# One-bank accumulators and four raw weight tiles in the MLP of an encoder layer

## The chip, the cores and the metric

The kernel runs on one core of a Trainium2 chip, in float32. TensorE (PE) multiplies; VectorE (DVE), ScalarE (ACT) and GpSimd (POOL) read and write tiles in on-chip memory; SyncE (SP) issues most of the DMA transfers, in the order of its queue. Each engine takes its instructions in order and waits on semaphores that other engines set. Accumulators lie in PSUM, which holds eight banks of 128 x 512 floats. The metric is the device time of one execution, in microseconds, as the median of several runs.

## The reference

One layer of an encoder over 1024 tokens of width 1024: windowed attention and a two-way SSD branch, merged by gates; cross attention; a squared-ReLU MLP of width 4096; a last RMSNorm. The change touches what follows the cross attention:

```python
    h = rmsnorm(x, norm_ffn[i])
    x = x + jnp.square(jax.nn.relu(h @ w_up[i])) @ w_down[i]
return rmsnorm(x, norm_final)
```

## The kernel before

**Precision.** Every product is made in three passes: an operand is split in a high part (ACT copies it in a rounded type) and a low part (the difference, by POOL or DVE), and PE adds high x high, high x low and low x high. `put` (L1071) splits one 128 x 512 piece of weights so: ACT at L1073, POOL at L1074; its result is a tile `wop`, of which there are six.

**The up projection** makes u = relu(h @ w_up) squared, 1024 x 4096, in 16 blocks of 256 columns. A block is a 2 x 2 product of halves (tokens, depth, columns), made with seven products in place of eight, in the manner of Strassen and Winograd. The left operands are `a11`, `a12`, `a22` and four sums `s1` to `s4`, made once. The right ones are sums of the block's raw weights b11, b21, b12, b22, which come by DMA in two tiles `raw` of 128 x 1024 (L1079, two buffers). `weights(b)` (L1082) makes them: DVE forms w0 and w1 (L1089, L1090), then overwrites w1 (L1096) and w0 (L1093) when `put` has read them. Each of the seven products is 12 matmuls of 128 x 128 by 128 x 512 (`product`, L1100).

**Order.** From the MLP on, PE's order is the order of the code; the other engines' order, and that of SP's queue, is set by a scheduler. The stage has three parts:

- *Products ahead* (`ahead`, L1117): for blocks 0 to 7 products 1 and 2 are made while the rows of h still come in, between the last units of the cross attention's output projection (`xops`), the transposes of rows (`nt`) and the sums (`sums`, L1033). Product 1 is copied to `x` (ACT, L1126) and stored; product 2 is added to it (DVE, L1129) for the quarter c11, and `square` (L1108) stores that. `x` is needed again later.
- *Whole quads* (`quad`, L1133): blocks 8 to 15, products 1, 2, 6, 5, 7, 3, 4. Product 1 is copied to c11 (ACT, L1147), product 2 added (DVE, L1149). Products 6, 7 and 4 add up in `pb`, products 5 and 3 in `pc`, each copied or added out between (L1153 to L1175).
- *Early quads*: blocks 0 to 7 in the same function, without products 1 and 2; `x` comes back by DMA (L1143). Product 6 in pb is added to x by DVE (c12, L1154) before product 7 adds on in the same tile. The last quarter c21 is L1171.

While quad n runs, the weights of quad n + 1 are made. In the last three rounds of the loop (n = 13 to 15 and behind it) the four u tiles and four tiles of w_down for the first block of the down projection are fetched (`uraw`, `draw`) and split (L1002 to L1014) into freed tiles `kt`. These raw rows lie in tiles of the tag `ld` (two buffers), which until the products ahead hold normalised rows `xn`.

**Accumulators.** Pool `pg` has two tiles of two banks each, pool `pp` four of one bank. In a block, `pc` and `pd` (products 5 and 2) are the halves of one two-bank tile, named `pcd`; in the products ahead the two products are its halves too. A wait is for a tile: who writes a half waits for the readers of that tile before it, whichever half they read. `pb`, `nt`, `xops` and, in the down projection, `dps` are of pool `pp`.

**The down projection** (L1179) adds u @ w_down to x in eight blocks over depth; a unit of 12 matmuls fills one `dps` tile, which DVE adds to the row (`xl`, L1215).

## Time and profile before

| | us |
|---|---|
| median of 3 runs | 2543.43 (2537.66 to 2545.66) |
| the profiled execution | 2546.5 |
| its span, first to last instruction | 2544.7, granted TensorE clock 0.984 on average |
| PE busy | 2421.6 (95%) |
| DVE, ACT, POOL busy | 1337.0, 1072.0, 1055.8 |
| products ahead, from the first product to the first whole quad | 1792.01 to 1876.55 |
| whole quads | to 2046.09 |
| early quads | to 2185.62 |
| down projection and last norm | to the end |

In rows of PE's timeline stand the start, the duration, the line and operation, the output and inputs by name, the number of matmuls taken together, and in brackets the idle time before with the engine and line that ended it. A matmul's duration includes its way through the array, so that rows overlap a little. PEclk is the share of the full clock that TensorE was granted. A list of waits gives for each line the engine and line that it waited for, the total, the number and the longest.

### The profile page before, as it was taken

To read this page: it belongs to the slowest core of one execution; us is meant where nothing else is said; L and a number is where in the kernel's file an instruction comes from. 1 tells how busy PE (TensorE), PEld (TensorE's weight loads), DVE (VectorE), ACT (ScalarE), POOL (GpSimd) and SP (SyncE) were. 2 spreads that over 40 slices of the span, in tenths; PEclk is the share of its full clock that TensorE was granted. 3 is DMA by queue.
4 is the path that set the end of the run, shared out by engine and by line. 5 is a ranking of instruction groups with operands and counts; after the bars stand their busy time and mean duration, and the time that the engine had idled before them with its cause. 6 is when DMAs were issued, how large, how long until landed. Compare 5 with 4: busy or idle time off the path is not lost.

```text
span 2544.7 us, 32517 instructions
## 1 busy us (share of the span) xinstructions
PE 2421.6 (95%) x12156; PEld 2002.4 (79%) x12156; DVE 1337.0 (53%) x2048; ACT 1072.0 (42%) x2214; POOL 1055.8 (41%) x905
## 2 busy tenths in 40 slices
PE   7899999999999999999999999999889998999998
PEld 6788887887878778777778788888767776788887
DVE  5747657576565752665552423236644465454443
ACT  5436445464453643776752422235433332221211
POOL 4234536345363442554444443244745544231210
PEclk9999999999999999999999999999989999999999
DMA  6213224132231311111153535122423344432211
GB/s 221 84 61 113 81 77 123 52 116 72 81 112 64 121 60 65 50 45 48 40 196 128 207 132 199 50 83 84 131 94 107 100 165 145 153 132 83 84 65 67
DMA packets 154926, 260.47 MB, mean 102 GB/s; under 512 B 11792, under 2 KB 86672, under 8 KB 154768
## 3 DMA queue, kind: packets, MB, share of 16 engines
q1 hardware_dynamic: 83872, 219.58, 25.3%
q10 hardware_dynamic: 70896, 38.81, 5.4%
q8 instruction: 96, 1.57, 0.2%
q14 instruction: 62, 0.51, 0.1%
HBM read 210.90 MB, written 47.45 MB: 102 GB/s over the span
## 4 chain that ended last, share of the span: by engine, by line
PE 62%; DVE 12%; POOL 8%; ACT 7%; issue 6%; DMA 4%; SPq 0%; ACTq 0%; POOLq 0%; DVEq 0%
PE dps L81 4%; PE dps L85 4%; PE dps L86 4%; PE pcd L1105 4%; PE pb L1105 4%; PE mps L86 3%; PE mps L85 3%; PE mps L81 3%; PE zp L85 2%; PE zp L81 2%; PE zp L86 2%; DMA raw<-in_wup_dram 2%; PE st L462 2%; POOL prev L477 1%; DVE cx L350 1%
## 5 line engine op out<-in xcount | busy, mean ns | idle before, releaser
L67 POOL TENSOR_TENSOR wlo<-raw,whi 128x1024 fp32r<-128x1024 f32 x142 | 349.8, 2464 | 599.0 <-ACT whi L66 566.4
L66 ACT ACTIVATE whi<-raw 128x1024 fp32r<-128x1024 f32 x144 | 152.0, 1055 | 257.6 <-PE mps L85 116.3
L81 PE MATMUL cps<-kt,whi 128*128 128x512 f32 x512 | 217.5, 425 | 8.6 <-DVE cx L350 8.6
L86 PE MATMUL cps<-kt,wlo 128*128 128x512 f32 x512 | 201.7, 394 | 0.0
L85 PE MATMUL cps<-kt,whi 128*128 128x512 f32 x512 | 201.4, 393 | 0.0
L1074 POOL TENSOR_TENSOR wop<-w,wop 128x512 fp32r<-128x512 f32 x64 | 92.1, 1445 | 117.6 <-ACT wop L1073 117.6
L81 PEld LDWEIGHTS cps<-kt,whi 128*128 128x128 f32 x512 | 97.4, 190 | 34.8 <-issue 16.0
L85 PEld LDWEIGHTS cps<-kt,whi 128*128 128x128 f32 x512 | 97.5, 191 | 26.1 <-issue 7.0
L86 PEld LDWEIGHTS cps<-kt,wlo 128*128 128x128 f32 x512 | 97.4, 190 | 21.1
L81 PE MATMUL gps<-kt,whi 128*128 128x512 f32 x256 | 109.6, 428 | 0.0
L120 POOL TENSOR_TENSOR rr<-rv,mhalf 128x1 f32<-128x1 f32 (+1 forms) x50 | 38.6, 772 | 171.1 <-DVE rv L118 165.7
L496 ACT ACTIVATE ef<-rows,ebias 128x128 f32<-128x128 f32 x256 | 83.2, 391 | 53.3 <-PE cb L511 49.6
L86 PE MATMUL mps<-yk,wlo 128*128 128x512 f32 x256 | 100.5, 393 | 4.8 <-POOL wlo L67 4.8
L680 POOL TENSOR_SCALAR t<-t,den 128x384 f32<-128x384 f32 (+1 forms) x128 | 69.2, 561 | 81.9 <-DVE den L678 73.7
L81 PE MATMUL dps<-kt 128*128 128x512 f32 x256 | 99.7, 390 | 2.7 <-DVE xl L1215 2.7
L86 PE MATMUL gps<-kt,wlo 128*128 128x512 f32 x256 | 101.8, 398 | 0.0
L1105 PE MATMUL pcd<-s,wop 128*128 128x512 f32 x384 | 95.9, 398 | 5.8 <-DVE c L1149 5.5
L85 PE MATMUL mps<-yk,whi 128*128 128x512 f32 x256 | 100.4, 392 | 0.8 <-DVE yk L734 0.8
L85 PE MATMUL gps<-kt,whi 128*128 128x512 f32 x256 | 101.2, 395 | 0.0
L81 PE MATMUL mps<-yk,whi 128*128 128x512 f32 x256 | 100.5, 393 | 0.0
L85 PE MATMUL dps<-kt 128*128 128x512 f32 x256 | 99.6, 389 | 0.0
L86 PE MATMUL dps<-kt 128*128 128x512 f32 x256 | 99.6, 389 | 0.0
(369 smaller groups left out, 7130.5 us busy)
## 6 DMA issues: line engine op xcount, KB each, us to landing
rows<-d_cs ACTq DMA_DIRECT2D x128, 256.0 KB, 3.8
raw<-in_wssd_dram SPq DMA_DIRECT2D x48, 512.0 KB, 3.3
raw<-in_wup_dram SPq DMA_DIRECT2D x40, 512.0 KB, 3.6
raw<-in_wsb_dram SPq DMA_DIRECT2D x32, 512.0 KB, 3.2
d_u<-c SPq DMA_DIRECT2D x64, 256.0 KB, 2.7
uraw<-d_u SPq DMA_DIRECT2D x32, 512.0 KB, 4.2
raw<-in_wdn_dram SPq DMA_DIRECT2D x28, 512.0 KB, 4.2
x<-in_x_dram SPq DMA_DIRECT2D x16, 512.0 KB, 6.4
```

Of the source, the lines that this page charges most:

```text
L66: nc.scalar.activation(hi, raw, AF.Copy)
L67: (eng or nc.gpsimd).tensor_tensor(lo, raw, hi.bitcast(F32), ALU.subtract)
L81: i = mm(out, l[0], r[0], start=first, stop=False)
L85: mm(out, l[0], r[1], start=False, stop=False)
L86: mm(out, l[1], r[0], start=False, stop=last)
L120: nc.gpsimd.tensor_tensor(r[:, :n], v[:, :n], kx.mhalf[:, :n], ALU.pow)
L350: V.scalar_tensor_tensor(acc[:, :S - o], ps[:, o:], cw(k), acc[:, :S - o], ALU.mult, ALU.add)
L462: PE.matmul(st[:, lo:hi], q.btok[:, c], xs.rearrange("p d h q -> p (d h q)")[:, lo:hi], start=True, stop=True)
L496: A.activation(ef[:, h], rows[:, 0, h], AF.Exp, bias=kx.ebias[:, b, j, 0, o:o + 1])
L680: G.tensor_scalar(t4[:, i, :n], t4[:, i, :n], den[:, i:i + 1], 1.0, ALU.mult, ALU.mult)
L1074: self.kx.nc.gpsimd.tensor_tensor(t[:, 1], src, t[:, 0].bitcast(F32), ALU.subtract)
L1105: self.kx.nc.tensor.matmul(ps, w[:, i, ks], act[:, k, j], start=start and k == 0 and m == 0, stop=k == 3 and m == 2, skip_group_check=True)
```

## The change

The two PSUM pools are closed where the MLP begins, and one pool `p8` of eight one-bank tiles, released tile by tile, is opened. All accumulators from there on are taken from it in turn: `xops`, `nt`, `pb`, `pc`, `pd`, `dps`. `pc` and `pd` are tiles of their own, and in the products ahead the two products go to `pb` and `pd`. The raw weights of every second block (the second, fourth and so on in the order 8 to 15, 0 to 7) go to the two `ld` tiles, so that raw weights have four tiles. Line numbers rise by three from `raw` on (by two in the second half of `quad`).

```diff
-            w = up.weights(order[0])
+            w = up.weights(order[0], False)
             for n, b in enumerate(order):
-                nxt = up.weights(order[n + 1]) if n < 15 else None
+                nxt = up.weights(order[n + 1], n % 2 == 0) if n < 15 else None
...
-    def raw(self, m):
-        r = self.kx.wp.tile([P, 1024], F32, tag="raw", bufs=self.kx.raw_bufs, name="raw")
+    def raw(self, m, spare=False):
+        if spare:
+            r = self.mp.tile([P, D], F32, tag="ld", bufs=2, name="raw")
+        else:
+            r = self.kx.wp.tile([P, 1024], F32, tag="raw", bufs=self.kx.raw_bufs, name="raw")
...
-    def weights(self, b):
+    def weights(self, b, spare):
...
-        b11, b21 = self.raw(2 * b)
-        b12, b22 = self.raw(2 * b + 1)
+        b11, b21 = self.raw(2 * b, spare)
+        b12, b22 = self.raw(2 * b + 1, spare)
...
-            cd = kx.pg.tile([P, S], F32, tag="g", name="pcd")
+            pb, pd = (kx.pp.tile([P, 512], F32, tag="p", name=n) for n in ("pb", "pd"))
             x, c11 = self.t2("x"), self.t2("c11")
-            self.product(cd[:, :512], w[1], 1, True)
-            kx.nc.scalar.activation(x, cd[:, :512], AF.Copy)
+            self.product(pb, w[1], 1, True)
+            kx.nc.scalar.activation(x, pb, AF.Copy)
             kx.nc.sync.dma_start(self.dr.u[2 * b + 1][:, :512], x)
-            self.product(cd[:, 512:], w[2], 2, True)
-            kx.nc.vector.tensor_tensor(c11, x, cd[:, 512:], ALU.add)
+            self.product(pd, w[2], 2, True)
+            kx.nc.vector.tensor_tensor(c11, x, pd, ALU.add)
...
-        pb = kx.pp.tile([P, 512], F32, tag="p", name="pb")
-        cd = kx.pg.tile([P, S], F32, tag="g", name="pcd")
-        pc, pd = cd[:, :512], cd[:, 512:]
+        pb, pc = (kx.pp.tile([P, 512], F32, tag="p", name=n) for n in ("pb", "pc"))
...
             c11 = self.t2("c11")
+            pd = kx.pp.tile([P, 512], F32, tag="p", name="pd")
...
-    kx.pg = ctx.enter_context(tc.tile_pool(name="pg", bufs=2, space=PSUM))
-    kx.pp = ctx.enter_context(tc.tile_pool(name="pp", bufs=4, space=PSUM))
+    psum = ExitStack()
+    kx.pg = psum.enter_context(tc.tile_pool(name="pg", bufs=2, space=PSUM))
+    kx.pp = psum.enter_context(tc.tile_pool(name="pp", bufs=4, space=PSUM))
...
         ok, grow = merge_cross_phase(kx, ins, dr, x1_open)
+        psum.close()
+        kx.pp = ctx.enter_context(tc.tile_pool(name="p8", bufs=8, space=PSUM, reuse_waits="tile"))
```

On PE the instructions and their order stay; their tiles change. These are the last products ahead and the first whole quad before, where `kt` stands for a11, a12 and s2, `s` and `a` for the other left operands:

```order
L1105 MATMUL pcd<-kt,wop 128x512 x48
L1105 MATMUL pb<-kt,wop 128x512 x12
L1105 MATMUL pcd<-kt,wop 128x512 x12
L1105 MATMUL pb<-kt,wop 128x512 x12
L1105 MATMUL pcd<-s_16131,wop 128x512 x12
L1105 MATMUL pb<-s_16132,wop 128x512 x12
L1105 MATMUL pcd<-s_16133,wop 128x512 x12
L1105 MATMUL pb<-a_16134,wop 128x512 x12
```

The same place on PE in the changed kernel:

```order
L1108 MATMUL pb<-kt,wop 128x512 x12
L1108 MATMUL pd<-kt,wop 128x512 x12
L1108 MATMUL pb<-kt,wop 128x512 x12
L1108 MATMUL pd<-kt,wop 128x512 x12
L1108 MATMUL pb<-kt,wop 128x512 x12
L1108 MATMUL pd<-kt,wop 128x512 x12
L1108 MATMUL pb<-kt,wop 128x512 x12
L1108 MATMUL pc<-s_16136,wop 128x512 x12
L1108 MATMUL pb<-s_16137,wop 128x512 x12
L1108 MATMUL pc<-s_16138,wop 128x512 x12
L1108 MATMUL pb<-a_16139,wop 128x512 x12
```

The 48 matmuls of two blocks into pcd are four products into four tiles now, and products 2 and 5 of the quad go to pd and pc.

ACT's queue at the start of the whole quads, before; `x_16676` and `x_16716` are the copies of blocks 6 and 7, `w0_16751`, `w1_16752` and `raw_16749` belong to block 8, the first whole quad, and `raw_16778` to block 9; `c11_16812` is the copy of block 8's product 1:

```order
L1126 ACTIVATE x_16676<-pcd_16675 128x512
L1052 ACTIVATE s4_16133<-f4_16649 128x4x128
L1126 ACTIVATE x_16716<-pcd_16715 128x512
L1073 ACTIVATE wop_16761<-w1_16752 128x512
L1073 ACTIVATE wop_16764<-w0_16751 128x512
L1073 ACTIVATE wop_16768<-w0_16751 128x512
L1073 ACTIVATE wop_16771<-raw_16749 128x512
L1073 ACTIVATE wop_16775<-w1_16752 128x512
L1073 ACTIVATE wop_16784<-raw_16778 128x512
L1147 ACTIVATE c11_16812<-pb_16809 128x512
```

The same place in the changed kernel; block 8 has `w0_16764`, `w1_16765` and `raw_16762`, block 9 `raw_16791` in an `ld` tile:

```order
L1129 ACTIVATE x_16688<-pb_16686 128x512
L1052 ACTIVATE s4_16138<-f4_16660 128x4x128
L1129 ACTIVATE x_16729<-pb_16727 128x512
L1073 ACTIVATE wop_16774<-w1_16765 128x512
L1073 ACTIVATE wop_16777<-w0_16764 128x512
L1149 ACTIVATE c11_16825<-pb_16822 128x512
L1073 ACTIVATE wop_16781<-w0_16764 128x512
L1073 ACTIVATE wop_16784<-raw_16762 128x512
L1073 ACTIVATE wop_16788<-w1_16765 128x512
L1073 ACTIVATE wop_16797<-raw_16791 128x512
```

The copy to c11 has moved ahead of three pieces of block 8 and one of block 9. On SP the two transfers of block 9's raws have moved from behind the last store of the products ahead (of u for block 7) to places among them: the first stands ahead of the store of block 3's c11, the second behind the store of block 5's x; they wait for the transposes that read the rows which lay in the `ld` tiles. Later on, the raws of each block are issued about one quad earlier than before.

DVE in the second early quad, from c21 of the first one on, before; `uraw` rows are splits of u for the down projection, w are sums of raw weights:

```order
L1171 TENSOR_TENSOR c_17916<-x,pb 128x512
L1089 TENSOR_TENSOR w_17968<-raw 128x512
L1090 TENSOR_TENSOR w_17969<-raw,w_17968 128x512
L1096 TENSOR_TENSOR w_17969<-raw,w_17969 128x512
L1093 TENSOR_TENSOR w_17968<-raw 128x512
L1154 TENSOR_TENSOR c_17991<-x,pb 128x512
L1154 TENSOR_TENSOR c_18019<-x,pcd 128x512
L1164 TENSOR_TENSOR c_18019<-c_18019,pb 128x512
L1109 SCALAR_TENSOR_TENSOR c_18019<-c_18019 128x512
L1007 TENSOR_TENSOR kt<-uraw,kt 128x512 x2
L1167 TENSOR_TENSOR c_17991<-c_17991,pcd 128x512
L1007 TENSOR_TENSOR kt<-uraw,kt 128x512
```

DVE in the fifth early quad of the changed kernel, from c12 on, with the start of the sixth:

```order
L1156 TENSOR_TENSOR c_18324<-x,pb 128x512
L1156 TENSOR_TENSOR c_18352<-x,pc 128x512
L1007 TENSOR_TENSOR kt<-uraw,kt 128x512
L1166 TENSOR_TENSOR c_18352<-c_18352,pb 128x512
L1007 TENSOR_TENSOR kt<-uraw,kt 128x512
L1112 SCALAR_TENSOR_TENSOR c_18352<-c_18352 128x512
L1169 TENSOR_TENSOR c_18324<-c_18324,pc 128x512
L1112 SCALAR_TENSOR_TENSOR c_18324<-c_18324 128x512
L1007 TENSOR_TENSOR kt<-uraw,kt 128x512
L1173 TENSOR_TENSOR c_18353<-x,pb 128x512
L1092 TENSOR_TENSOR w_18405<-raw 128x512
L1007 TENSOR_TENSOR kt<-uraw,kt 128x512
```

Up to the fifth early quad no split stands in DVE's queue any more; the first splits of u come here, three quads later than before, and some of them between c21 and the w's. The order c21, four w's, c12 within a quad is the same in both kernels.

## The prediction

> **What bounds the kernel now.** I read the busy time of stretches first, then the waits of TensorE (PE) over the stages that the change touches, then PE's timeline where the waits stand. The stretches, from the window view (us; busy time of each engine; last PEclk, DMA share, GB/s):

> ```profile
> core 0: us, PE busy (x) PEld busy (x) DVE busy (x) ACT busy (x) POOL busy (x), PEclk, DMA share, GB/s
> 1792.00:1877.00 85.00, 69.11 (x324) 56.16 (x323) 50.61 (x60) 34.03 (x59) 56.60 (x39) 0.90 0.37 121
> 1890.00:2047.00 157.00, 151.49 (x648) 121.23 (x647) 66.29 (x81) 53.22 (x92) 78.72 (x53) 1.00 0.32 105
> 2047.00:2193.00 146.00, 127.82 (x510) 100.77 (x509) 78.82 (x99) 44.56 (x70) 58.43 (x38) 0.93 0.45 151
> 2300.00:2400.00 100.00, 100.00 (x443) 82.81 (x442) 44.39 (x53) 17.28 (x24) 20.04 (x8) 1.00 0.25 84
> ```

> They are the products made ahead, the whole quads, the early quads, and a piece of the down projection. PE is the bound in all four, and only in the last one is it always busy: what the change can win lies in PE's gaps in the first three. Their causes, from the waits of PE over 1700 to 2545 us (total, times, longest):

> ```profile
> PE pcd L1105 <- ACT x L1126: 15.9, 8, 4.5
> PE pb L1105 <- ACT wop L1073: 11.7, 5, 2.7
> PE pb L1105 <- DVE c L1154: 6.2, 3, 5.1
> PE pcd L1105 <- DVE c L1149: 5.5, 7, 1.0
> PE pb L1105 <- ACT c L1147: 5.4, 1, 5.4
> PE dps L81 <- DVE xl L1215: 2.7, 1, 2.7
> PE xops L81 <- DVE x L924: 1.8, 1, 1.8
> ```

> Rows 1 and 4 are of one kind: one half of a two-bank tile is ready for PE, but it waits for a reader of the other half. Rows 6 and 7 are four one-bank tiles run out. Rows 2, 3 and 5 are the supply of split weights, and c12 and c11 behind it.

> **Products ahead.** PE's timeline (start, duration, form; the idle time before in brackets):

> ```profile
> 1792.01 2.91 PE L1105 MATMUL pcd<-kt,wop 128*128 128x512 f32 x12
> 1795.65 3.03 PE L1105 MATMUL pcd<-kt,wop 128*128 128x512 f32 x12 [0.74 <-ACT x L1126]
> 1812.53 4.55 PE L1105 MATMUL pcd<-kt,wop 128*128 128x512 f32 x12 [4.49 <-ACT x L1126]
> 1828.90 7.34 PE L1105 MATMUL pcd<-kt,wop 128*128 128x512 f32 x24 [2.45 <-ACT x L1126]
> 1846.30 7.36 PE L1105 MATMUL pcd<-kt,wop 128*128 128x512 f32 x24 [2.74 <-ACT x L1126]
> 1864.35 8.60 PE L1105 MATMUL pcd<-kt,wop 128*128 128x512 f32 x24 [3.32 <-ACT x L1126]
> 1876.55 2.88 PE L1105 MATMUL pb<-kt,wop 128*128 128x512 f32 x12
> 1887.57 4.58 PE L1105 MATMUL pb<-kt,wop 128*128 128x512 f32 x12 [5.41 <-ACT c L1147]
> ```

> A product is 12 matmuls: 2.9 us alone, 5.64 for two in a row (2.74 from start to start, below, and the second's 2.9). The stage runs from 1792.01 to 1876.55, 84.5 us. In it lie the 15.9 us of eight waits and the slow matmuls behind them, at half clock: 4.55 for 2.91 is 1.64, 7.34 and 7.36 for 5.64 are 1.70 and 1.72, 8.60 for 5.64 is 2.96, together 8.0. Without both, 60.6 us are left. With separate tiles the second product needs only its weights and a tile that was used eight tiles before. POOL, which makes the low parts, has 56.6 us of work here (first window), and waits for ACT's high parts now and then, so it comes within 4 us of PE's 60.6 and will show. I take a stage of 63, **21.5 us gained**; the ends are 24 (PE alone bounds) and 10 (POOL and ACT stay as idle as now in half of the stage).

> Gaps as short as 2.45 us are followed by slow matmuls here, and no matmul is slow that has no such gap before it or before its neighbour; so I count the slow time as the gap's, and it goes with the gap. [...]

> **Start of the whole quads.** Product 6 of the first (1887.57) waits 5.41 us and then runs 1.7 slow (4.58 for 2.9): 7.1 in all. It adds into pb, which ACT must first copy to c11, and ACT's queue says why that is late:

> ```profile
> 1886.40 0.63 ACT L1073 ACTIVATE wop<-raw 128x512 fp32r<-128x512 f32 x1 [0.93 <-DMA raw<-in_wup_dram]
> 1886.94 0.58 ACT L1147 ACTIVATE c<-pb 128x512 f32<-128x512 f32 x1
> ```

> The copy stood behind the next block's wop, whose raw had no tile before. In the changed order it stands behind two wop only, which need nothing but block 8's own raws, and block 9's come early in tiles of their own. SP's queue holds those two transfers until the last transposes, with stores behind them that nobody waits for soon. I take **6**, between 0 (another wait on ACT takes its place) and 7.1.

> **Whole quads.** Product 5 (first into pc) waits for DVE's c11 of the neighbour half in seven of eight quads, 5.5 us, and each restart costs some 0.1 (3.03 against 2.91 in the first two rows above): **6 gained**. What is late next is the weights of product 6; PE's 151.49 busy of 157 leaves nothing else. POOL has 78.7 of 157, so the supply can follow. Ends 4 and 7.

> **Early quads.** PE again: first and last start of the eight, and the stalled products 7:

> ```profile
> 2046.09 2.91 PE L1105 MATMUL pb<-kt,wop 128*128 128x512 f32 x12
> 2048.83 2.96 PE L1105 MATMUL pcd<-s,wop 128*128 128x512 f32 x12
> 2052.65 3.05 PE L1105 MATMUL pb<-s,wop 128*128 128x512 f32 x12 [0.86 <-DVE c L1154]
> 2069.32 3.03 PE L1105 MATMUL pb<-s,wop 128*128 128x512 f32 x12 [2.50 <-ACT wop L1073]
> 2086.19 5.46 PE L1105 MATMUL pb<-s,wop 128*128 128x512 f32 x12 [2.70 <-ACT wop L1073]
> 2108.18 5.14 PE L1105 MATMUL pb<-s,wop 128*128 128x512 f32 x12 [5.07 <-DVE c L1154]
> 2126.63 4.51 PE L1105 MATMUL pb<-s,wop 128*128 128x512 f32 x12 [2.18 <-ACT wop L1073]
> 2144.24 3.02 PE L1105 MATMUL pb<-s,wop 128*128 128x512 f32 x12 [1.95 <-ACT wop L1073]
> 2160.79 4.48 PE L1105 MATMUL pb<-s,wop 128*128 128x512 f32 x12 [2.41 <-ACT wop L1073]
> 2185.62 0.40 PE L81 MATMUL dps<-kt 128*128 128x512 f32 x1
> ```

> Product 7 adds into pb, which c12 has to read first, and c12 stands in DVE's queue behind the next block's weights. That is not changed. The gaps shown are 17.7 us, the slow matmuls 2.5, 2.2, 1.55 and 1.5 (against 2.96), together 25.4. DVE's queue in the second quad:

> ```profile
> 2061.32 0.69 DVE L1171 TENSOR_TENSOR c<-x,pb 128x512 f32<-128x512 f32 x1 [1.38 <-PE pb L1105]
> 2062.66 0.69 DVE L1089 TENSOR_TENSOR w<-raw 128x512 f32<-128x512 f32 x1 [0.65 <-DMA raw<-in_wup_dram]
> 2063.39 0.69 DVE L1090 TENSOR_TENSOR w<-raw,w 128x512 f32<-128x512 f32 x1
> 2066.23 1.75 DVE L1096 TENSOR_TENSOR w<-raw,w 128x512 f32<-128x512 f32 x1 [2.16 <-POOL wop L1074]
> 2068.50 0.67 DVE L1154 TENSOR_TENSOR c<-x,pb 128x512 f32<-128x512 f32 x1
> 2078.95 0.67 DVE L1171 TENSOR_TENSOR c<-x,pb 128x512 f32<-128x512 f32 x1
> ```

> With four raws the 0.65 us wait for the transfer goes, and the rest of the chain stays: the gap of 2.50 becomes 1.85. In the third quad c21 ran at 2078.95 because four splits of u stood before it; these splits (ACT and DVE, for the first block of the down projection) move from quads 2 to 4 to quads 5 to 8, since the tiles they used hold raws now. So I count 0.9 for the first quad, 1.85 for the next four, 6 for the sixth (a case like the 5.07, with slow matmuls), 3 and 0.5 for the last two: 17.8 of 25.4 stay, **7.5 gained**. The ends are 14 (the moved splits find room) and -3 (they cost in four quads what they cost in three).

> **Ends of the chain.** The 1.8 us for xops and the 2.7 for dps go with eight tiles in place of four: four more products of 2.74 lie between a tile and its next use; **4.5**, ends 0 and 4.5. The rest of the down projection is at 100.00 of 100 and gives nothing. A wait of a tile for its reader eight tiles before isn't in the trace: from 0 to one product, 2.74, in all; I take 0, since the longest wait for a reader just before (5.1) is shorter than four products. Four raws in flight are bounded by 0 and by the late transfer of 0.65 us in each of eight quads, 5; I take 0.

> **Sum.** 21.5 + 6 + 6 + 7.5 + 4.5 = 45.5 us. The profiled execution took 2546.5 us (span 2544.7), 3.1 above the median of 2543.4: 2546.5 - 45.5 = 2501.0 in its terms, 2498 in the median's.

> **Rivals.**
> - *Supply takes over in the products ahead.* POOL's 56.6 us and ACT's in-order queue hold PE: 10 there and 2 at the start of the quads in place of 21.5 and 6: 2498 + 15.5 = 2513. For it: POOL's share; against: 4 us of room. 0.18.
> - *Moved splits cost.* -3 in place of 7.5 in the early quads: 2508. For it: DVE's queue is the chain there; against: DVE has 78.8 of 146 us. 0.14.
> - *Slow matmuls have another cause than the short gaps*, and only those behind the gaps of 4.49, 5.07 and 5.41 us go: 1.70, 1.72 and 2.96 ahead stay, and of the early ones that I count as gone some 4: 2498 + 10 = 2508. Against it: the gaps before each of them. 0.04. [...]
> - *The change doesn't do what it says*: the tiles are still given back together, and a product still waits for its neighbour's reader. Then only the late transfers are won, 8 times 0.65 us, 2538. Against it: the names are separate tiles of a pool that is said to be released by tile. 0.04.
> - *Slower: raws and splits block each other.* The u splits of the last four early quads need tiles that raws hold, the last block's raws wait for these splits, and in SP's queue the stores of c12 and c21 and the loads of x stand behind them. I count 1.85, 6, 3 and 0.5 for these quads, 11.35. If each lost L, the time would be 2498 - 11.35 + 4 L: not below 2543 from L = 14.1 on, and 2555 at 17. The worst one now, with splits in it, loses 5.07 + 2.2 = 7.3, and SP has a whole quad of over 14 us (2046.09 to 2061.12 is one) for two transfers. 0.03.

> **Numbers.** The forecast itself, 2490 to 2504, has 0.54; 0.03 lies below it, to the ends of 24, 7.1, 7, 14 and 4.5 (57 us, 2486). The rivals at 2508 to 2513 have 0.36 and can come together: 45.5 - 15.5 - 10.5 = 19.5, 2524, at little weight. Range 2486 to 2517. This kernel's runs differ by about 0.3%, so faster by more than that is below 2536: 0.93, all but the last two rivals; the fourth is the same, 0.04, and the last slower, 0.03.

> **What would show it.** Right: in the list of PE's waits none for x or c11 in the products ahead and the whole quads; product 1 of the first whole quad at 1852 to 1858, POOL over 85% busy before it, whole quads about 19.6 us apart, gaps of 1.9 without slow matmuls in quads 2 to 5. Wrong: products ahead that wait for wop; product 6 waiting 5 us at the first whole quad; early quads over 17.5 us on average; PE idle at the first dps.

## The result, and the profile after

The changed kernel takes 2502.58 us (median of 4 runs, 2500.91 to 2504.38) against 2544.55 us before (2537.66 to 2545.7): a ratio of 0.9841 with a 95% interval of 0.9821 to 0.9860, or 42 us less. The forecast was 2498, with 2486 to 2517 as its range.

The profiled execution took 2500.91 us, its span is 2499.1. Where the time went, by the starts of the stages on PE's timeline (us):

| stage | before | after | gained | forecast |
|---|---|---|---|---|
| to the last transposes in the cross attention (`xpt`) | 1758.02 | 1752.76 | 5.3 | not touched |
| from there to the first product | 33.99 | 31.93 | 2.1 | 1.8 |
| products ahead | 84.54 | 59.66 | 24.9 | 21.5 |
| first whole quad | 27.14 | 26.55 | 0.6 | 6 |
| the other seven | 142.40 | 135.57 | 6.8 | 6 |
| early quads | 139.53 | 136.59 | 2.9 | 7.5 |
| from the first dps to the end | 359.08 | 356.04 | 3.0 | 2.7 |

The first row is no work of the change. It lies in code that the diff leaves alone; in the profile of before PE waited 4.8 us for POOL once in the branch projections (`mps`), in this one 0.3, and over all profiled executions of this study that place is reached between 1752.6 and 1761.1. Without it the traces differ by 40.3 us.

PE's waits from 1776 to 2143 us in the changed kernel (total, times, longest):

```profile
PE pb L1108 <- ACT wop L1073: 13.7, 6, 4.8
PE pb L1108 <- ACT c L1149: 3.6, 1, 3.6
PE pb L1108 <- DVE c L1156: 1.6, 1, 1.6
PE pb L1108 <- DVE c L1166: 1.0, 1, 1.0
PE pb L1108 <- POOL wop L1074: 0.4, 1, 0.4
```

The waits for x (15.9) and for c11 (5.5) have no row any more. What stands first is the supply of weights. PE's timeline at both ends of the products ahead, and the busy time between:

```profile
1784.69 2.91 PE L1108 MATMUL pb<-kt,wop 128*128 128x512 f32 x12
1787.44 2.88 PE L1108 MATMUL pd<-kt,wop 128*128 128x512 f32 x12
...
1844.35 2.88 PE L1108 MATMUL pb<-kt,wop 128*128 128x512 f32 x12
1847.07 2.88 PE L1108 MATMUL pd<-kt,wop 128*128 128x512 f32 x12
1853.60 5.02 PE L1108 MATMUL pb<-kt,wop 128*128 128x512 f32 x12 [3.65 <-ACT c L1149]
```

```profile
core 0: us, PE busy (x) PEld busy (x) DVE busy (x) ACT busy (x) POOL busy (x), PEclk, DMA share, GB/s
1784.70:1844.30 59.60, 59.15 (x322) 50.68 (x321) 47.01 (x56) 32.79 (x57) 54.42 (x36) 1.00 0.48 156
```

PE is busy for 59.15 of 59.60 us at full clock; POOL for 54.42, 91% of it, and it keeps up. The bill comes at the start of the whole quads: product 6 of the first one waits 3.65 us. DVE and ACT just ahead of it:

```profile
1844.86 0.68 DVE L1053 TENSOR_TENSOR a<-nt,a 128x512 fp32r<-128x512 f32 x1
1845.70 0.69 DVE L1132 TENSOR_TENSOR c<-x,pd 128x512 f32<-128x512 f32 x1 [0.16 <-ACT s L1052]
1846.42 1.47 DVE L1112 SCALAR_TENSOR_TENSOR c<-c 128x512 f32<-128x512 f32 x1
1847.81 0.68 DVE L1132 TENSOR_TENSOR c<-x,pd 128x512 f32<-128x512 f32 x1
1848.41 1.19 DVE L1092 TENSOR_TENSOR w<-raw 128x512 f32<-128x512 f32 x1
1849.52 1.75 DVE L1112 SCALAR_TENSOR_TENSOR c<-c 128x512 f32<-128x512 f32 x1
1851.20 0.68 DVE L1093 TENSOR_TENSOR w<-raw,w 128x512 f32<-128x512 f32 x1
```

```profile
1851.91 1.15 ACT L1073 ACTIVATE wop<-w 128x512 fp32r<-128x512 f32 x2 [5.05 <-DVE w L1093]
1852.97 0.58 ACT L1149 ACTIVATE c<-pb 128x512 f32<-128x512 f32 x1
```

DVE runs with a single gap of 0.16 us from the last sums through c11 of the last two blocks to w1 of block 8, which ends 7.5 us after product 1 of this quad began (1851.88 against 1844.35). ACT waits 5.05 us for it, and the copy that frees pb stands behind.

The early quads, PE's stalled products 7:

```profile
2027.88 4.58 PE L1108 MATMUL pb<-s,wop 128*128 128x512 f32 x12 [1.79 <-ACT wop L1073]
2045.37 4.58 PE L1108 MATMUL pb<-s,wop 128*128 128x512 f32 x12 [1.78 <-ACT wop L1073]
2062.87 3.02 PE L1108 MATMUL pb<-s,wop 128*128 128x512 f32 x12 [1.78 <-ACT wop L1073]
2078.80 4.51 PE L1108 MATMUL pb<-s,wop 128*128 128x512 f32 x12 [1.78 <-ACT wop L1073]
2099.29 5.10 PE L1108 MATMUL pb<-s,wop 128*128 128x512 f32 x12 [4.76 <-ACT wop L1073]
2117.29 4.58 PE L1108 MATMUL pb<-s,wop 128*128 128x512 f32 x12 [1.77 <-ACT wop L1073]
2134.61 3.02 PE L1108 MATMUL pb<-s,wop 128*128 128x512 f32 x12 [1.65 <-DVE c L1156]
```

The gaps are as forecast (1.85; the sixth over 4), but four of the five gaps near 1.78 have slow matmuls behind them, and one has not. The gap of 4.76 us has this before it, on ACT and on DVE:

```profile
2090.09 1.15 ACT L1006 ACTIVATE kt<-uraw 128x512 fp32r<-128x512 f32 x2 [3.18 <-DMA uraw<-d_u]
```

```profile
2090.75 0.69 DVE L1007 TENSOR_TENSOR kt<-uraw,kt 128x512 fp32r<-128x512 f32 x1 [3.10 <-ACT kt L1006]
2091.36 0.68 DVE L1173 TENSOR_TENSOR c<-x,pb 128x512 f32<-128x512 f32 x1
```

Here c21, and the next block's weights behind it, stand in DVE's queue behind a split of u, the split waits for ACT's copy, and the copy waits for the transfer of the u row.

### The profile page after: what moved, and what is told of

Same layout as the page of the kernel before. It is cut to its first block, busy times and chain, and to the rows that moved or that the text cites. A ratio compares the mean times of both kernels' runs of the same rounds, so it can differ in the third digit from the quotient of the medians.

```text
span 2499.1 us, 32531 instructions
## 1 busy us (share of the span) xinstructions
PE 2409.9 (96%) x12156; PEld 1998.4 (80%) x12156; DVE 1357.4 (54%) x2048; ACT 1072.5 (43%) x2214; POOL 1054.1 (42%) x905
## 4 chain that ended last, share of the span: by engine, by line
PE 64%; DVE 13%; POOL 8%; ACT 7%; issue 6%; DMA 2%; SPq 0%; ACTq 0%; POOLq 0%; DVEq 0%
PE pb L1108 5%; PE dps L85 5%; PE dps L86 5%; PE dps L81 5%; PE mps L85 3%; PE mps L86 3%; PE mps L81 3%; PE zp L85 2%; PE zp L81 2%; PE zp L86 2%; PE pc L1108 2%; PE st L462 2%; DVE cx L350 2%; POOL prev L477 2%; POOL cb_t L476 1%
## 5 line engine op out<-in xcount | busy, mean ns | idle before, releaser
L81 PE MATMUL cps<-kt,whi 128*128 128x512 f32 x512 | 217.9, 426 | 8.6 <-DVE cx L350 8.6
L1074 POOL TENSOR_TENSOR wop<-w,wop 128x512 fp32r<-128x512 f32 x64 | 92.9, 1458 | 94.0 <-ACT wop L1073 94.0
L81 PEld LDWEIGHTS cps<-kt,whi 128*128 128x128 f32 x512 | 97.5, 190 | 35.0 <-issue 16.3
L81 PE MATMUL gps<-kt,whi 128*128 128x512 f32 x256 | 108.8, 425 | 0.0
L680 POOL TENSOR_SCALAR t<-t,den 128x384 f32<-128x384 f32 (+1 forms) x128 | 69.1, 559 | 82.0 <-DVE den L678 62.9
L81 PE MATMUL mps<-yk,whi 128*128 128x512 f32 x256 | 99.9, 390 | 0.0
L85 PE MATMUL dps<-kt 128*128 128x512 f32 x256 | 99.7, 389 | 0.0
L81 PE MATMUL dps<-kt 128*128 128x512 f32 x256 | 99.7, 389 | 0.0
L85 PE MATMUL dps<-wd,u 128*128 128x512 f32 x256 | 99.7, 389 | 0.0
L86 PE MATMUL dps<-wd,u 128*128 128x512 f32 x256 | 99.7, 389 | 0.0
```

The source lines that it names most:

```text
L81: i = mm(out, l[0], r[0], start=first, stop=False)
L85: mm(out, l[0], r[1], start=False, stop=False)
L86: mm(out, l[1], r[0], start=False, stop=last)
L680: G.tensor_scalar(t4[:, i, :n], t4[:, i, :n], den[:, i:i + 1], 1.0, ALU.mult, ALU.mult)
L1074: self.kx.nc.gpsimd.tensor_tensor(t[:, 1], src, t[:, 0].bitcast(F32), ALU.subtract)
```

## The experiments

All runs by stage, from the same places on PE's timeline as above; "p6" is the time from the first product ahead to product 6 of the first whole quad. The stages are those of one profiled execution; the ratio is to the kernel before in the same set of runs, so ratios are compared across sets, not medians.

| run | ahead | first quad | p6 | seven quads | early | rest | median us | ratio to before, interval |
|---|---|---|---|---|---|---|---|---|
| before | 84.5 | 27.1 | 95.6 | 142.4 | 139.5 | 359.1 | 2544.55 | |
| changed | 59.7 | 26.6 | 68.9 | 135.6 | 136.6 | 356.0 | 2502.58 | 0.9841 (0.9821 to 0.9860) |
| accumulators alone | 59.9 | 32.6 | 76.0 | 135.6 | 136.7 | 356.1 | 2514.19 | 0.9876 (0.9853 to 0.9900) |
| raws alone | 84.6 | 21.8 | 90.0 | 135.6 | 130.1 | 362.5 | 2527.57 | 0.9934 (0.9908 to 0.9960) |
| four and four | 61.3 | 24.8 | 68.8 | 135.6 | 130.8 | 360.8 | 2506.26 | 0.9838 (0.9811 to 0.9864) |
| one spare pair | 59.7 | 26.8 | 69.3 | 135.6 | 136.6 | 356.1 | 2506.67 | 0.9850 (0.9834 to 0.9866) |
| squares on ACT | 62.9 | 21.9 | 68.4 | 135.6 | 131.4 | 356.0 | 2499.37 | 0.9821 (0.9806 to 0.9836) |
| own tile for 7 | 59.6 | 26.7 | 69.0 | 135.6 | 119.5 | 356.1 | 2488.77 | 0.9777 (0.9754 to 0.9800) |
| + splits on POOL | 59.8 | 26.5 | 69.0 | 135.6 | 119.7 | 356.1 | 2489.24 | 0.9779 (0.9763 to 0.9795) |
| + squares too | 63.1 | 23.2 | 68.6 | 135.6 | 120.6 | 356.1 | 2488.09 | 0.9780 (0.9760 to 0.9799) |
| own tile, spares to 12 | 59.8 | 26.5 | 69.1 | 135.6 | 121.5 | 356.1 | 2488.23 | 0.9778 (0.9764 to 0.9791) |
| + two squares | 59.6 | 25.5 | 68.3 | 135.6 | 120.8 | 356.1 | 2490.63 | 0.9789 (0.9774 to 0.9803) |
| own tile, u rows in pairs | 59.7 | 26.7 | 69.2 | 135.6 | 124.5 | 356.1 | 2492.57 | 0.9797 (0.9776 to 0.9817) |
| changed, again | 59.6 | 26.1 | 69.0 | 135.6 | 129.6 | 356.1 | 2498.72 | 0.9818 (0.9796 to 0.9840) |

### Accumulators alone

```diff
-                nxt = up.weights(order[n + 1], n % 2 == 0) if n < 15 else None
+                nxt = up.weights(order[n + 1], False) if n < 15 else None
```

> Eight one-bank tiles alone, raw weights in two tiles as before. Theory A (the halves of one tile were the wait in the products ahead and the whole quads; the raws only move work in the early quads): products ahead as in the changed kernel, first whole quad begins about 60 us after the first product; a whole quad takes 19.4 us; early quads as before, 139 us in all, with the splits of u in quads 2 to 4; time about 2507, 4 to 5 us above the changed kernel. Theory B (the spare raws feed the products ahead and the start of the quads too): products ahead over 65 us, time 2513 or more.

The products ahead (59.9), the whole quads (19.4 each) and the early quads came as theory A had them, the time as B had it: 2514. Neither had the place. PE (first row) and ACT in this run:

```profile
1864.76 5.46 PE L1108 MATMUL pb<-kt,wop 128*128 128x512 f32 x12 [10.53 <-ACT c L1149]
```

```profile
1856.49 1.15 ACT L1073 ACTIVATE wop<-w 128x512 fp32r<-128x512 f32 x2 [4.96 <-DVE w L1093]
1860.86 0.63 ACT L1073 ACTIVATE wop<-w 128x512 fp32r<-128x512 f32 x1 [3.22 <-DVE w L1096]
...
1863.59 0.63 ACT L1073 ACTIVATE wop<-raw 128x512 fp32r<-128x512 f32 x1 [1.06 <-DMA raw<-in_wup_dram]
1864.13 0.58 ACT L1149 ACTIVATE c<-pb 128x512 f32<-128x512 f32 x1
```

The wait before product 6 grows from 5.41 to 10.53 us. The copy to c11 stands behind five pieces of block 8 and one of block 9, in the order that ACT had in the kernel before, while PE arrives earlier: a part of the gain ahead is given back at once. Of ACT's time there, the transfer of block 9's raw takes only 1.06 us. More goes with the wait of 3.22 us for a later weight of block 8, behind which the copy would not stand in the changed kernel's order. So by these rows the early raws act mainly through ACT's order.

### Raws alone

The four edits to `raw` and `weights` on the kernel before, whose accumulators stay:

```diff
-            w = up.weights(order[0])
+            w = up.weights(order[0], False)
-                nxt = up.weights(order[n + 1]) if n < 15 else None
+                nxt = up.weights(order[n + 1], n % 2 == 0) if n < 15 else None
```

> Four raw tiles alone, accumulators as before. Theory A: waits for x (16 us) and c11 (5.5 us) on PE stay; only the early quads change, by about 3 us; time about 2541. Theory B: the supply was a bound of its own; products ahead below 80 us and time under 2533.

A miss for A: 2527.6, 18 us below before. Theory B has the time (under 2533) but not the place, since the products ahead take 84.6 us. The wait for x stays (16.0 us in this run's list of waits), but the one for c11 is gone and each whole quad takes 19.4 us, with the shared tile still there. The reason is in DVE's queue, first in the kernel before:

```profile
1909.92 0.69 DVE L1089 TENSOR_TENSOR w<-raw 128x512 f32<-128x512 f32 x1 [7.10 <-DMA raw<-in_wup_dram]
1910.65 1.67 DVE L1090 TENSOR_TENSOR w<-raw,w 128x512 f32<-128x512 f32 x1
1912.24 0.67 DVE L1149 TENSOR_TENSOR c<-c,pcd 128x512 f32<-128x512 f32 x1
```

and c11 in this run:

```profile
1898.68 0.69 DVE L1152 TENSOR_TENSOR c<-c,pcd 128x512 f32<-128x512 f32 x1 [2.61 <-PE pcd L1108]
```

Before, c11 stood behind two w's that waited 7.10 us for a transfer; with the raw there early it waits only for its product. So product 5 was late because of the shared tile and the late raw together, and either part of the change takes the 6.8 us away. The first quad has no wait before product 6 here: 21.8 us against 27.1 before, with PE as late as before and only the raws earlier. The early quads fall by 9.4 us, where A had 3: their gaps before product 7 are 1.75 to 1.79 us with no slow matmuls behind them, but for the sixth quad. The rest is 3.4 us longer, with a wait of 3.3 us at the first dps.

### Four and four

```diff
-            pb, pd = (kx.pp.tile([P, 512], F32, tag="p", name=n) for n in ("pb", "pd"))
+            pb, pd = (kx.pg.tile([P, 512], F32, tag="g", name=n) for n in ("pb", "pd"))
...
-        pb, pc = (kx.pp.tile([P, 512], F32, tag="p", name=n) for n in ("pb", "pc"))
+        pb = kx.pp.tile([P, 512], F32, tag="p", name="pb")
+        pc = kx.pg.tile([P, 512], F32, tag="g", name="pc")
...
-            pd = kx.pp.tile([P, 512], F32, tag="p", name="pd")
+            pd = kx.pg.tile([P, 512], F32, tag="g", name="pd")
...
-        kx.pp = ctx.enter_context(tc.tile_pool(name="p8", bufs=8, space=PSUM, reuse_waits="tile"))
+        kx.pg = ctx.enter_context(tc.tile_pool(name="g4", bufs=4, space=PSUM, reuse_waits="tile"))
+        kx.pp = ctx.enter_context(tc.tile_pool(name="p4p", bufs=4, space=PSUM, reuse_waits="tile"))
```

> The change, but the accumulators in two pools of four one-bank tiles: pc, pd (and the pair of the products ahead) in one, pb, xops, nt and dps in the other. Theory A (separate tiles for the halves do it, the number in turn only covers the two ends): products ahead and whole quads as in the changed kernel, the waits of xops (1.8) and dps (2.7) come back; time about 2507. Theory C (eight tiles in one turn are what PE runs ahead on): the pair of the products ahead waits for c11 of two blocks earlier, over 5 us of waits ahead, time 2512 or more.

As A had it: 2506.3 against 2507. The waits at the two ends are back:

```profile
1783.15 0.66 PE L148 MATMUL nt<-ident,xn 128*128 128x128 f32 x4 [1.76 <-DVE x L924]
...
2156.63 0.50 PE L81 MATMUL dps<-kt 128*128 128x512 f32 x1 [2.90 <-DVE xl L1218]
```

The products ahead lose 1.6 us to two more short waits of xops. It is the separation that does it; eight tiles in one turn are worth some 6.7 us in this trace: 2.0 before the first product, 1.6 ahead and 4.8 behind the first dps, less 1.7 at the first quad. The early quads, 5.9 us shorter than in the changed kernel's first profile, are left out: the changed kernel's second profile (129.6) is shorter there too.

### Own tile for product 7

```diff
+        pe = self.kx.pp.tile([P, 512], F32, tag="p", name="pe")
+        self.product(pb, w[6], 6, True)
+        V.tensor_tensor(x, x, pb, ALU.add)
+        self.product(pc, w[5], 5, True)
...
+        V.tensor_tensor(c22, x, pc, ALU.add)
+        self.product(pe, w[7], 7, True)
+        V.tensor_tensor(c22, c22, pe, ALU.add)
...
+        self.product(pc, w[3], 3, False)
+        V.tensor_tensor(c12, x, pc, ALU.add)
...
+        self.product(pe, w[4], 4, False)
+        V.tensor_tensor(c21, x, pe, ALU.add)
...
```

> The change, and in the early quads product 7 goes to a tile of its own (pe), with x + product 6 kept in x; as many operations on DVE as before. Theory A (product 7 waits for c12, which stands in DVE's queue behind the next block's weights, and the slow matmuls come from that gap): the gaps of 1.8 us before product 7 and the slow matmuls behind them go, 24 us less perhaps 4 that stay where splits of u stand in the queue; time about 2483. Theory D (the queue itself is the bound and the wait only moves to product 3, which waits for c22 behind the same weights): gaps over 1 us before product 3, time 2494 or more.

The early quads fall to 119.5 us (eight at full speed without a gap are 111.4, 13.92 each, as the first one takes in the changed kernel from 2006.47 to 2020.39), 17.1 less than in the changed kernel's first profile and 10.1 less than in its second; the time falls to 2488.8. Theory A's mechanism holds: no wait before product 7. The time is 6 us above A's 2483, in part because PE still stands in the sixth quad, now before product 3 (this run, PE and ACT):

```profile
2092.45 2.90 PE L1108 MATMUL pc<-s,wop 128*128 128x512 f32 x6 [4.94 <-DVE c L1190]
```

```profile
2081.69 1.15 ACT L1006 ACTIVATE kt<-uraw 128x512 fp32r<-128x512 f32 x2 [5.36 <-DMA uraw<-d_u]
```

### Squares on ACT

```diff
-            self.square(c11, b, 0, 0)
+            kx.nc.scalar.activation(c11, c11, AF.Relu)
+            kx.nc.scalar.activation(c11, c11, AF.Square)
+            kx.nc.sync.dma_start(self.dr.u[2 * b][:, :512], c11)
```

> The change, with the squares of c11 in the products ahead as Relu and Square on ACT in place of one operation on DVE. Theory A (the wait of 3.65 us before product 6 of the first whole quad is DVE's queue of sums, c11 and squares in front of the first weights, of which the last two squares are 3.2 us): that wait falls to 1 us or less and the slow matmuls behind it go; the first whole quad takes about 21 us in place of 26.5; time about 2498. Theory E (the queue of ACT and POOL behind it is as late): the wait stays over 3 us, time 2502 or more.

The wait before product 6 is gone and the first quad takes 21.9 us, as A said; but the products ahead take 3.3 us more:

```profile
1827.53 1.97 PE L1044 MATMUL nt<-ident,xn 128*128 128x128 f32 x8 [2.73 <-DVE rv L118]
```

Product 6 begins 68.4 us after the first product, in place of 68.9, and by the end of the first quad 1.4 us is won. More lies in the early quads (131.4 in place of 136.6), and the changed kernel's second set (2498.72) has that too. The new wait is for the norm of the last rows: ACT starts their sum of squares (`xn`) 31.3 us after the first product in place of 27.4. So a wait of nearly the same size came up earlier, and this run alone doesn't show that DVE's queue made the first one.

### One spare pair

```diff
-                nxt = up.weights(order[n + 1], n % 2 == 0) if n < 15 else None
+                nxt = up.weights(order[n + 1], n == 0) if n < 15 else None
```

> The change, with the two spare raw tiles used for block 9 alone. Theory G (with separate accumulators the spare raws matter only at the start, where block 9's weights stood in ACT's queue ahead of the copy to c11 and waited for their transfer): first whole quad about 26.5 us as in the changed kernel and not 32.6 as with the accumulators alone; whole quads 19.4; early quads 133 to 139 with the splits of u in quads 2 to 4; time 2499 to 2506. Theory B (they feed the whole stage): whole quads over 19.6 or the first one over 30, time 2508 or more.

Stage by stage as theory G had it, at 2506.7 (G's range ended at 2506). With one pair the first quad is 26.8 in place of 32.6: beside separate accumulators, block 9's raws are where the spare tiles pay first. The early quads take as long as in the changed kernel's first profile (136.6) and 7 us longer than in its second (129.6). The other spare pairs shorten the gaps before product 7 there: they are 2.1 to 2.7 us in this run, 5.10 in the fourth quad, against 1.78 in the changed kernel. How much of that shows in the time depends on the slow matmuls behind the gaps, which the last run bears on.

### Splits on POOL, all three, spares to 12, two squares, u rows in pairs

Five attempts at what is left, all on the kernel with the own tile. The splits' low parts on POOL:

```diff
-                        split_u(kx, dr, us, j, raw)
+                        split_u(kx, dr, us, j, raw, nc.gpsimd)
...
-        nc.vector.tensor_tensor(t[:, 1], rh, t[:, 0].bitcast(F32), ALU.subtract)
+        (eng or nc.vector).tensor_tensor(t[:, 1], rh, t[:, 0].bitcast(F32), ALU.subtract)
```

> As with product 7 in a tile of its own, and the low parts of the eight u splits in the early quads on POOL in place of DVE. Theory A (the 4.9 us before product 3 in the sixth early quad are the splits in DVE's queue): that wait falls below 2 us, early quads from 119.5 to about 114 us, time about 2484. Theory F (POOL, which makes the weights' low parts that DVE waits for, takes over): a wait over 3 us stays in the sixth or seventh early quad, time 2488 or more.

The wait stays (5.68 us before product 3 of the sixth quad), though no split is left in DVE's queue, and 2489.2 is the outcome that theory F forecast. So splits in DVE's queue are not needed for it. F's mechanism shows in part: DVE waits 5.88 us for POOL, whose splits end 1.0 us after the high part that it needs next, but ACT is late first. The next block's w1 is ready at 2085.46 and ACT takes it at 2088.53, behind its copies of u rows and two operations on c21:

```profile
2085.55 1.15 ACT L1006 ACTIVATE kt<-uraw 128x512 fp32r<-128x512 f32 x2 [5.34 <-DMA uraw<-d_u]
```

With the squares on ACT as well:

> Product 7 in a tile of its own, squares of the products ahead on ACT, u splits on POOL. Theory A: the three gains add, time about 2479, 9 to 10 us below the one with the own tile alone. Theories E and F: 2487 or more.

2488.1, as theories E and F had it: the gains didn't add. The u rows earlier, by leaving the `ld` tiles to them from n = 12 on:

```diff
-                nxt = up.weights(order[n + 1], n % 2 == 0) if n < 15 else None
+                nxt = up.weights(order[n + 1], n % 2 == 0 and n < 12) if n < 15 else None
```

> Product 7 in a tile of its own, and the spare raw tiles used for the first six odd blocks of the order only (n below 12), so that the u rows of the down projection find the ld tiles free two quads earlier. Theory H (the wait of 4.9 us in the sixth early quad is ACT's, which stands at the head of its queue for the transfer of a u row that was issued late because its tile held raws): the wait goes, early quads from 119.5 to 114 us or less, time about 2483. Theory A' (it is the number of splits in one quad, wherever it lies): a wait over 3 us turns up in the fourth or fifth early quad, time 2487 or more.

The wait moved to the fourth quad (4.99 us), as A' had it, and ACT's wait for a u row, 5.53 us at 2052.62, moved with it.

The same with the squares of c11 on ACT for blocks 6 and 7 alone (the edit of "Squares on ACT", as the other branch of `if b < 6`):

> As the run before, and the squares of c11 of blocks 6 and 7 alone on ACT. Theory A (DVE's queue holds the first weights up): the wait before product 6 of the first whole quad falls from 3.7 to under 1.5 us, without the wait for the rows' norm that came when all eight squares were on ACT; 4 us less than the run before, time about 2479. Rival: a wait of the same size turns up at the next product, no gain.

The wait before product 6 is 3.08 in place of 3.62 us. There is no gain, as the rival had it, though the wait is still before the same product. Without its last two squares DVE isn't busy throughout any more:

```profile
1854.50 0.69 DVE L1132 TENSOR_TENSOR c<-x,pd 128x512 f32<-128x512 f32 x1 [1.91 <-ACT x L1129]
```

Now it waits for ACT's copy of product 1, which stands behind the square of block 6 on ACT. So DVE's queue alone isn't the cause of the late start; what it would be with the squares out of both queues was not tried. And the u rows in two pairs:

```diff
-                if n == 13:
-                    us = down_us(kx)
-                    for j in range(4):
+                if n in (11, 13):
+                    us = down_us(kx) if n == 11 else us
+                    for j in range(n - 11, n - 9):
```

> Product 7 in a tile of its own, all spare pairs kept, and the u rows of the down projection fetched in two pairs, at n = 11 and n = 13, each pair behind the splits that free both ld tiles. ACT's copies of a u row now stand behind the two copies of new weights in their quads. Theory H (what is left in the early quads is ACT standing at the head of its queue for a u row that was issued late): no wait over 2 us in the early quads, which take 114 us or less in all; time about 2483. Theory A' (so many splits cost it wherever they lie): a wait over 3 us stays, time 2487 or more.

Two waits now, 4.04 us in the fourth quad and 2.98 in the sixth, and 2492.6: again the case of A', a wait over 3 us and a time above 2487. ACT waits 5.35 us for a u row in the fourth quad.

In every one of the five runs a wait of PE in the early quads stays and goes where the u rows go. For theory H speak ACT's rows: with the spare raws in use, ACT stands for the transfer of a u row just ahead of each such wait. The splits alone don't make it, which speaks against A'. In the kernel before, the accumulators alone and the run with one spare pair, ACT waits 0.5 us at most for a u row; four pieces of u in the second quad are followed there by a gap of 2.67 to 2.71 us, hardly more than the gap before that (2.24 to 2.50). In this run's fourth quad two pieces go with 4.04. But H isn't shown by an experiment either: both forecasts made from it failed, and the two waits don't go together in size (3.18 us on ACT and 4.76 on PE in the changed kernel, 5.36 and 4.94 with the own tile, 4.26 and 2.98 in the sixth quad of this run). Nor is a u row's transfer the only thing that makes such a wait. In the same three runs the fourth quad has one of 5.05 to 5.10 us; there two pieces of w_down stand in ACT's queue, in the kernel before:

```profile
2100.49 1.04 ACT L1013 ACTIVATE kt<-draw 128x1024 fp32r<-128x1024 f32 x1
...
2103.51 1.06 ACT L1013 ACTIVATE kt<-draw 128x1024 fp32r<-128x1024 f32 x1 [0.93 <-DMA draw<-in_wdn_dram]
```

Tiles of their own for the u rows were not tried. What placement would be free of the wait stays open.

### The changed kernel again

> The changed kernel once more, beside the run before on the same chip: 2500 to 2505. If slow matmuls behind gaps of 1.8 us depend on where the gap lies against the clock's steps, the same quads can have them or not in this execution while the gaps stay 1.77 to 1.79; if it is the gap's length alone, the same four quads have them.

The gaps in quads 2 to 5 are 1.77 to 1.79 as before, and no matmul behind them is slow; the early quads take 129.6 us in place of 136.6. One of the gaps, and the steps of the granted clock around it, in this execution and in the first (PE's row; then the windows of 3.41 us, PEclk third from the end):

```profile
2033.58 3.02 PE L1108 MATMUL pb<-s,wop 128*128 128x512 f32 x12 [1.79 <-ACT wop L1073]
```

```profile
2029.59:2033.00 3.41, 2.20 (x10) 1.44 (x8) 2.54 (x3) 0.21 (x2) 2.09 (x2) 1.00 0.08 28
2033.00:2036.41 3.41, 2.83 (x12) 2.37 (x13) 1.03 (x2) 0.56 (x1) 1.30 (x1) 1.00 0.46 154
```

```profile
2021.92:2025.33 3.41, 3.41 (x17) 2.77 (x16) 1.25 (x2) 1.93 (x4) 1.89 (x2) 1.00 0.42 157
2025.33:2028.75 3.42, 1.63 (x8) 1.04 (x7) 3.00 (x4) 0.63 (x1) 1.47 (x2) 1.00 0.34 122
2028.75:2032.16 3.41, 3.41 (x10) 2.63 (x9) 0.00 (x0) 0.00 (x0) 0.47 (x1) 0.50 0.08 31
```

In the first execution (lower fence) the gap of 1.79 us lies in one step, PE is busy for 1.63 of 3.42 us, and the next step is at half clock from end to end. In the second (upper fence) the same gap is split over two steps, 2.20 and 2.83 us busy, and the clock stays. So it is not the gap's length alone. The time, 2498.7, is a little below the 2500 to 2505 expected.

## Why the prediction was right

The forecast of 45.5 us stands against 42.0 in the medians and 40.3 in the traces. The main step, that PE waits in the products ahead for a reader of the other half and that separate tiles end this, is shown. That the total came so near is in part luck: by stages, 3.4 too little ahead stands against 5.4 too much at the first quad and, in the first profile, 4.6 too much in the early quads. Point by point:

- **Ends of the chain** (4.5): 2.1 and 3.0, and four tiles in place of eight bring both waits back (1.76 and 2.90 us).
- **Products ahead** (21.5): 24.9. The mechanism is shown by the accumulators alone (59.9 us) and the raws alone (84.6). The size was off because I let POOL show in the stage itself; it kept up. The slow matmuls went with the gaps: the stage has a granted clock of 1.00.
- **Start of the whole quads** (6): 0.6. The step that failed is "it stands behind two wop only, which need nothing but block 8's own raws": they need DVE too, whose w1 comes 7.5 us after product 1 began. I had read the old wait as one for block 9's raw, but ACT waited only 0.93 us for that; the copy also stood behind later pieces of block 8, for one of which ACT waited 3.27 us (at 1883.80, in the kernel before). The rival of the supply was right in this place alone (2 by it, 0.6 measured), through DVE and ACT and not POOL. Both terms together, 27.5, came to 25.5. In all eleven runs with separate accumulators and a spare pair, the two of the changed kernel among them, product 6 begins 68.3 to 69.3 us after the first product, wherever the squares ran; PE's own work up to there is 65.1 (59.6 and two products of 2.74). What sets the other 3 to 4 us is not shown beyond the queues of DVE and ACT, which both stood in the way in one run or another.
- **Whole quads** (6): 6.8, but for half of the reason. I gave the wait to the shared tile; the late raw was the other condition, and either edit removes it.
- **Early quads** (7.5): 2.9 in the profile beside the forecast, 9.9 in the second. The chain and its gap of 1.85 were right (1.77 to 1.79), and product 7's wait is shown by the own tile, which removes it. One step failed: "1.85 for the next four" left out that such a gap can be followed by slow matmuls, 1.6 us (4.58 against 2.96) in four quads of the first profile. The sixth quad's loss had the right size (6 forecast, 4.76 and 2.1 measured in the first profile), and it goes with the moved splits, as forecast. But it stays when DVE has no split left, and by the rows ACT's wait for a u row, which the prediction left out, is part of it; that cause is argued from the rows and not shown.
- **Rivals.** That moved splits cost is true for the sixth quad alone. That slow matmuls have another cause than short gaps did not come true in the products ahead, where the gaps are gone and the granted clock is 1.00 (0.90 before, over 1792 to 1877 us). The line that this rival drew, between gaps of 3.32 and 4.49 us, is shown by no run: in the kernel before, the gaps of 2.45 and 2.74 us have a step at half clock behind them (at 1829.50 and 1846.56). But a gap's length alone doesn't decide it: the same 1.79 us has half clock behind it where it lies in one step (PE busy for 1.63 of 3.42 us), and full clock where it is split over two (2.20 and 2.83 us busy).

The own tile for product 7 beats both kernels: 2488.8 us, 0.9777 of before. The five runs built on it with other edits don't differ from it beyond their intervals.

## What to carry to other kernels

A wait on an accumulator has two sides, who still has to read it and why that reader is late; separate tiles and earlier loads can each remove the same wait (here the 6.8 us of the seven quads), so their gains neither add nor can be told from the whole. When a fix lets the bounding engine arrive earlier, the next thing to read is the in-order queue of the engine that feeds its next step: 5.5 of the 25 us won here were lost there without the spare loads. And side work in an in-order queue (here the splits of u) may be moved from quad to quad and from engine to engine without its cost going away: wherever it was put here, a wait of 4.0 to 5.7 us stayed on PE.

## What the runs showed of the hardware

In DVE's rows above, one operation on 128 x 512 takes different times: L1093 0.68 us at 1851.20 in the changed kernel, and the same line, L1090 in the kernel before, 1.67 at 1910.65. The cause was not tried.
